# One decoder-layer step: all weight splits on VectorE and ScalarE, sample states loaded on ScalarE's queue, 32x32 products of two block pairs in turn

## The chip, the core and the metric

The kernel runs on one core of a Trainium2 chip. The metric is device time in microseconds (us) of one execution. The core has a matrix engine (TensorE, PE in the profile; its weight loads are PEld), three engines for elementwise work (VectorE or DVE, ScalarE or ACT, GpSimd or POOL) and a queue engine (SyncE, SP). SP and ACT both issue the DMAs of this kernel, each on a hardware queue of its own (q1 and q10 in the profile). Each engine works through its own instructions in order.

## The reference, cut to what matters

One layer of a decoder for a prompt of 256 tokens and 8 sample tokens, which share all weights. So every large product has 264 columns.

```python
h = rmsnorm(x, norm_mix); proj = h @ w_in
pool_out, pool_new = pool_mixer(proj[pool part], ...)          # windows 2/4/8/16
q, k, v = short_conv(proj[qkv part]); o, ssm_new = gated_delta_chunked(q, k, v, g, beta, ssm)
merged = gate_pool * (pool_out @ w_pool_up) + gate_gdn * (gdn_out @ w_gdn_up)
x = x + merged @ w_o
gu = rmsnorm(x, norm_ffn) @ w_gate_up
x = x + (silu(gu[..., :D_FF]) * gu[..., D_FF:]) @ w_down
x = x + (p_l @ w_ple) * sigmoid(x @ w_ple_gate)
# per chunk of gated_delta_chunked: solve (I + strictly lower A) X = rhs, then update the state S
# per sample: S = exp(g) S + k (beta (v - (exp(g) S)^T k))^T ; o = S^T q   (16 heads of 128x128, 8 samples)
```

All data are float32, and all weights (some 300 MB) are read once from HBM.

## The kernel before, in words

**Large products.** Activations lie channel by token. A float32 product is made of three fast ones: each operand is cut into a rounded part and a rest (`wh` and `wl` for a weight block, `hh` and `hl` and so on for activations), and `gemm` (L469) issues `wh*xh`, `wh*xl`, `wl*xh`, each a 128x128 weight tile against 264 columns, into one PSUM bank of tag `acc`. Such a product is called an acc matmul below.

**Weight stream.** `wload` (L429) issues a 512 KB DMA on SP into one of three `wr` buffers. `wsplit` (L441) makes `wh` as a copy on ACT (L355) and `wl` as a subtraction (L339), four buffers of each. `wblock` (L456) keeps up to three split blocks (`LA`) ahead of the matmuls, two more loaded (`LD`). A block feeds 24 acc matmuls. The subtraction of `wl` goes to DVE, except where the test `spare` of `wsplit` sends it to POOL: when the planner's clock of POOL is more than 1.0 us behind that of DVE and DVE's is more than 1.5 us ahead of PE's. Two blocks at the head of the program (in `input_norm`, L631) name POOL outright.

**Order of work.** The order on each engine is written out by the program itself. A planner (`Model`, L34) keeps a clock for each engine from a cost table. Small pieces of work are Python generators; `tick` (after 6 or so acc matmuls) lets the next piece emit its instructions when the planner says that its inputs are there (`at`), unless `behind` finds DVE or ACT more than `room` (3.0 us) ahead of PE. What is emitted is pinned in that order (`pin`). So a planner's estimate that is too early makes the in-order engine wait on the chip, and every later instruction with it.

**Small pieces that the change touches.** `gdn_b` (L1019) inverts the 128x128 triangular blocks of a head group from 32x32 blocks: `px` takes for each of 8 blocks a and for the two block pairs e = 0 and 2 a product of 32x32 blocks (L1060 to L1063), and `py` the same with two products for e = 0 and one for e = 2 (L1069 to L1075). Both write one PSUM bank. Each of these matmuls is float32 and stands as two instructions in the profile. There are four head groups.

`gdn_sample` (L1177) updates the 8 samples' states. A tile `S` holds one head of all samples (128 x 8 x 128, 512 KB) in four buffers. `load` (L1212) issues its DMA on SP; `kqmm` (L1256) waits in the planner for the state and emits 8 small matmuls (16 instructions, `kqp`, L1266); then `pd` products and DVE updates in place (`S`, L345); `swap` (L1217) stores the new state on SP, waits in the planner for the store's landing and calls `load` for the same head of the next group into the same buffer. 16 loads, 16 stores. The pooling mixer (`sw`, `dd`, `db` tiles on DVE) and the products with `w_pool_up` run at the same time.

Of the kernel before, what the change touches and what calls it, by code (L numbers as in the profile page):

```python
# [8 lines left out]
F32 = mybir.dt.float32  # L9
# [21 lines left out]
GH = 4  # L31


class Model:  # L34
# [4 lines left out]
    def __init__(self, nc):  # L39
        self.nc, self.seen, self.bb = nc, 0, None  # L40
        self.T = {e: 0.0 for e in ("PE", "DVE", "Activation", "Pool", "SP")}
        self.ring = 0.0
# [84 lines left out]
    def run(self, floor=0.0):  # L127
# [5 lines left out]
        for k in range(self.seen, len(lst)):  # L133
            i = lst[k]
            eng = str(i.engine).split(".")[-1]
            if eng not in self.T or type(i).__name__.startswith("Bass"):
                continue
            ins = [b for b in map(self.box, i.ins) if b]
            out = [b for b in map(self.box, i.outs) if b]
            at = max([self.T[eng], floor] + [self.ready(b) for b in ins])  # L140
            if type(i).__name__ == "InstDMACopy":
                self.T[eng] = at + 0.06
                n = max(self.free(b) * (b[2] - b[1]) for b in ins + out) * 4
# [10 lines left out]
            held, more = self.cost(i, ins, out)  # L154
            self.T[eng] = at + held
            end = at + held + more
# [7 lines left out]
class Step:  # L164
# [55 lines left out]
    @property  # L220
    def now(self):
        return self.model.T["PE"]

# [214 lines left out]
        self.note(self.splits[-3] if len(self.splits) > 2 else 0.0)  # L438
        self.raws.append((raw, nk, n))

    def wsplit(self, eng=None):  # L441
        self.note()
        raw, nk, n = self.raws.pop(0)
        hi, lo = (self.wp.tile([P, 1024], F32R, tag=t, name=self.nm(t))[:, :nk * n].rearrange("p (k c) -> p k c", c=n)
                  for t in ("wh", "wl"))
        self.nsp += 1
        self.copy(hi, raw)
        T = self.model.T
        spare = T["Pool"] + 1.0 < T["DVE"] and T["DVE"] - T["PE"] > 1.5
        self.sub(lo, raw, hi.bitcast(F32), self.nc.gpsimd if spare else eng)  # L450
        self.npool = getattr(self, "npool", 0) + spare
        self.pre.append((hi, lo))
        self.splits.append(self.note(self.now))

# [176 lines left out]
    def input_norm(self, x, xs):  # L631
        nc = self.nc
        ssq = self.cp.tile([P, 3, 4], F32, name="ssq")
        nc.vector.memset(ssq, 0.0)
        self.xt = self.B3("xT")
        sqj = self.e4("sqj")
        self.xd = self.dp.tile([P, KT, NT], F32, tag="xd", name="xd", bufs=1)
        self.hh = self.B3("hh", F32R)
        self.hl = self.B3("hl", F32R)
        self.xn = None  # L640

        def squares(c):
            cs = slice(c * 512, c * 512 + 512)
            xc = (c % 2) * 512
            self.act(sqj[:, :512], x[:, 0, cs], AF.Square, accum_out=ssq[:, 0, c:c + 1])
            for src, acc in ((x[:, 1, cs], ssq[:, 1, c:c + 1]),
                             (xs[c // 2][:, xc:xc + 512], ssq[:NS, 2, c:c + 1])):
                nc.vector.scalar_tensor_tensor(out=sqj[:src.shape[0], 512:1024], in0=src, scalar=1.0, in1=src,
                                               op0=ALU.mult, op1=ALU.mult, accum_out=acc)

        def turn(k):
            t = self.ps("xt")[:, :NT]
            for b in range(2):
                self.tr(t[:, b * P:(b + 1) * P], x[:, b, k * P:(k + 1) * P])
            cc = (k % 8) * P
            self.tr(t[:, TP:NT], xs[k // 8][:, cc:cc + P])
            if k % 4 == 3:
                nc.vector.tensor_copy(self.xt[:, k], t)
            else:
                self.copy(self.xt[:, k], t)  # L660
        self.turn = turn
        for k in range(12):
            if k in (0, 4, 8):
                squares(k // 4)
            if k == 10:
                squares(3)
            if k == 8:
                self.wsplit(nc.gpsimd)
            turn(k)
        r = self.cp.tile([P, 3], F32, name="rin")  # L670
        nc.vector.tensor_reduce(r, ssq, axis=AX.X, op=ALU.add)
        self.ts(r, r, 1.0 / D, EPS, ALU.mult, ALU.add)
        self.powr(r, r, -0.5)
        self.wsplit(nc.gpsimd)
        turn(12)
        p = self.spread_rows(r)
        turn(13)
        self.rx = self.e1("rx")
        self.copy(self.rx, p)
        for k in range(2):  # L680
            self.htile(k)
        self.wsplit()
        for k in range(2, 4):
            self.htile(k)
# [334 lines left out]
    def gdn_b(self, hg, q, k, v):  # L1019
        nc, gw, o = self.nc, self.gw, self.o  # L1020
        h0 = hg * GH
        G8 = 2 * GH
# [20 lines left out]
        for g in range(2):  # L1043
            for hh in range(2):
                for b in range(2):
                    h = 2 * g + hh
# [10 lines left out]

        sl = lambda i, n: slice(i * n, (i + 1) * n)
        px = self.ps("px").rearrange("p (a c) -> p a c", c=64)
        for e in (0, 2):  # L1060
            E, O = sl(e, 32), sl(e + 1, 32)
            for a in range(G8):
                self.mm(px[O, a, 0:32], A[E, a, O], Tm[E, a, E])  # L1063
        yield -1
        for e in (0, 2):
            O = sl(e + 1, 32)
            nc.vector.tensor_copy(X[O, :, 0:32], px[O, :, 0:32])
        yield -1
        py = self.ps("py").rearrange("p (a c) -> p a c", c=64)  # L1069
        for e in (0, 2):  # L1070
            E, O = sl(e, 32), sl(e + 1, 32)
            for a in range(G8):
                self.mm(py[E, a, 0:32], X[O, a, 0:32], Tt[O, a, O])
                if e == 0:
                    self.mm(py[O, a, 0:32], Tt[O, a, O], X[O, a, 0:32])  # L1075
        yield -1
        for e in (0, 2):
            E, O = sl(e, 32), sl(e + 1, 32)
# [4 lines left out]
        lo, hi = slice(0, 64), slice(64, 128)  # L1083
# [93 lines left out]
    def gdn_sample(self, pool):  # L1177
        nc, o = self.nc, self.o
# [31 lines left out]
        S = {}  # L1210

        def load(hg, h):  # L1212
            S[hg, h] = pool.tile([P, NS, HD], F32, tag="S", name=self.nm("S"), bufs=4)
            self.dma(S[hg, h], self.i["state_ssm"][0, :, hg * GH + h].rearrange("b d e -> d b e"))
        order = list(range(GH - 1, -1, -1))

        def swap(hg, h):  # L1217
            yield self.at(S[hg, h])
            self.dma(o["ssm_s"][0, :, hg * GH + h].rearrange("b d e -> d b e"), S.pop((hg, h)))
            if hg < 3:  # L1220
                yield "stored"
                load(hg + 1, h)
        for h in order:
            load(0, h)
# [31 lines left out]
        def kqmm(hg, h):  # L1256
            while (hg, h) not in S:
                yield -1
            yield self.at(S[hg, h])
            if h == order[0]:  # L1260
                self.kept.clear()
                kqp[0] = self.ps("kqp", True)
            for sl in (2 * h + 1, 2 * h):
                wd = 32 if sl == 7 else 16
                for j in range(4):
                    nc.tensor.matmul(kqp[0][32 * j:32 * j + wd, :P], kq[:, j, 16 * sl:16 * sl + wd],  # L1266
                                     S[hg, h][:, 4 * (sl % 2) + j, :], start=(sl == 7), stop=(sl == 0),
                                     tile_position=(0, 32 * j))
        for h in order:
            yield -1  # L1270
            yield from kqmm(0, h)
        yield -1
        for hg in range(4):
# [38 lines left out]
            for h in order:  # L1312
                for c in range(2):
                    pd = self.ps("pd").rearrange("p (b e) -> p b e", b=4)
                    self.mm(pd, ks[:, hg], rm[:, 4 * c:4 * c + 4, :])
                    if h:
                        mask(h - 1, c)
                    yield -1
                    for b in range(4):
                        bb = 4 * c + b  # L1320
                        n = hg * n32 + h * NS + bb
                        self.stt(S[hg, h][:, bb, :], S[hg, h][:, bb, :], egb[:, n:n + 1], pd[:, b, :])
                    yield 1.2
                self.lane(swap(hg, h))
                if hg < 3 and h < 2:
                    yield from kqmm(hg + 1, h + 2)
            if hg < 3:
                yield -1
                yield from kqmm(hg + 1, 1)
                yield -1  # L1330
                yield from kqmm(hg + 1, 0)
                yield -1
# [451 lines left out]
```

## Time and profile before

| | us |
|---|---|
| median of 3 runs (1927.98 to 1929.02) | 1928.94 |
| profiled execution, whole | 1929.83 |
| its span, first to last instruction | 1928.1 |
| PE busy | 1881.3 |
| DVE busy | 1128.0 |
| ACT busy | 880.9 |
| POOL busy | 521.2 |

The profiled execution is 1.7 us longer than its span and 0.9 us longer than the median of the runs. From about 830 us on (products with `w_gdn_up`, `w_o`, the feed-forward part) PE is busy with hardly a gap up to about 1830 us; the mixer, the gated delta rule and the sample states lie before that. PE's busy time counts overlapping matmuls, so a busy share of 100% says that no gap was seen, not that the array is at its peak.

### The profile page before, as it was taken

The numbers are of one execution on the slowest core, as the hardware profiler recorded it, in microseconds if no ns is written. First come the engines' busy times: TensorE is split into PE (matmuls) and PEld (weight loads), VectorE is DVE, ScalarE is ACT, GpSimd is POOL, SyncE is SP. The second block draws the span as 40 slices with busy tenths as digits, with TensorE's granted clock in tenths as the row PEclk, the third lists the DMA queues.
The fourth block names the chain that finished last, engine by engine and source line by source line (L and its number), as shares of the span: only waits on it lengthen the run. The fifth ranks groups of instructions, "written<-read, shape, count | busy, mean of one in ns | idle before, by whom it ended". The sixth has DMA issues, their size and how long they took to land.

```text
span 1928.1 us, 38025 instructions
## 1 busy us (share of the span) xinstructions
PE 1881.3 (98%) x15700; PEld 1853.6 (96%) x15700; DVE 1128.0 (59%) x1594; ACT 880.9 (46%) x1484; POOL 521.2 (27%) x560
## 2 busy tenths in 40 slices
PE   8999999999999799999999999999999999999997
PEld 6899999999999799999999999999999999999997
DVE  6756466546546866566665555544555545557554
ACT  4565657455544243344444444333444333444444
POOL 3347353622514443322232111100111001122211
PEclk9999999989999899999999999999999999999998
DMA  6556564645656778755655656555555655556553
GB/s 176 153 174 191 135 177 123 189 114 162 183 155 170 222 237 240 219 171 185 220 179 172 193 187 195 185 177 175 176 186 183 191 183 177 175 177 188 161 177 120
DMA packets 368817, 344.92 MB, mean 179 GB/s; under 512 B 26387, under 2 KB 363100, under 8 KB 368628
## 3 DMA queue, kind: packets, MB, share of 16 engines
q1 hardware_dynamic: 355011, 338.82, 58.1%
q10 hardware_dynamic: 13632, 3.67, 0.9%
q8 instruction: 123, 2.02, 0.4%
q14 instruction: 51, 0.41, 0.1%
HBM read 327.28 MB, written 16.03 MB: 178 GB/s over the span
## 4 chain that ended last, share of the span: by engine, by line
PE 85%; DVE 6%; DMA 4%; ACT 2%; issue 2%; POOL 1%; SPq 0%; ACTq 0%; POOLq 0%; DVEq 0%
PE acc L368 79%; DVE wl L339 1%; ACT wh L355 1%; DMA out_dram<-S 1%; DVE sw L336 1%; DMA S<-in_state_ssm_dram 1%; POOL wl L339 1%; DMA wr<-in_w_in_dram 1%; DVE k L345 1%; PE pp L368 0%; PE py L368 0%; PE kv L372 0%; PE px L368 0%; DVE S L345 0%; PE pS L368 0%
## 5 line engine op out<-in xcount | busy, mean ns | idle before, releaser
L339 DVE TENSOR_TENSOR wl<-wr,wh 128x1024 fp32r<-128x1024 f32 (+1 forms) x490 | 620.5, 1279 | 529.8 <-ACT wh L355 528.1
L355 ACT ACTIVATE wh<-wr 128x1024 fp32r<-128x1024 f32 x594 | 611.1, 1049 | 444.2 <-PE acc L368 161.4
L368 PE MATMUL acc<-hh,wh 128*128 128x264 f32 x1664 | 488.3, 293 | 3.7 <-DVE q L345 1.9
L368 PE MATMUL acc<-hl,wh 128*128 128x264 f32 x1664 | 478.2, 287 | 1.2 <-DVE hl L339 1.0
L368 PE MATMUL acc<-hh,wl 128*128 128x264 f32 x1664 | 477.0, 287 | 2.3 <-DVE wl L339 1.5
L339 POOL TENSOR_TENSOR wl<-wr,wh 128x1024 fp32r<-128x1024 f32 x104 | 256.6, 2470 | 705.8 <-ACT wh L355 425.0
L368 PE MATMUL acc<-xnh,wh 128*128 128x264 f32 x1408 | 399.9, 284 | 0.0
L368 PE MATMUL acc<-xnh,wl 128*128 128x264 f32 x1408 | 399.2, 283 | 0.0
L368 PE MATMUL acc<-xnl,wh 128*128 128x264 f32 x1408 | 399.1, 283 | 0.0
L368 PEld LDWEIGHTS acc<-hh,wh 128*128 128x128 f32 x1664 | 318.5, 191 | 8.0 <-issue 2.4
L368 PEld LDWEIGHTS acc<-hl,wh 128*128 128x128 f32 x1664 | 318.8, 192 | 3.7 <-DVE hl L339 2.4
L368 PEld LDWEIGHTS acc<-hh,wl 128*128 128x128 f32 x1664 | 317.7, 191 | 2.7 <-DVE wl L339 1.7
L368 PEld LDWEIGHTS acc<-xnl,wh 128*128 128x128 f32 x1408 | 265.1, 188 | 0.0
L368 PEld LDWEIGHTS acc<-xnh,wh 128*128 128x128 f32 x1408 | 264.8, 188 | 0.1
L368 PEld LDWEIGHTS acc<-xnh,wl 128*128 128x128 f32 x1408 | 264.4, 188 | 0.0
L368 PE MATMUL acc<-hidh,wh 128*128 128x264 f32 x704 | 199.9, 284 | 0.0
L368 PE MATMUL acc<-hidl,wh 128*128 128x264 f32 x704 | 199.6, 283 | 0.0
L368 PE MATMUL acc<-hidh,wl 128*128 128x264 f32 x704 | 199.5, 283 | 0.0
L368 PEld LDWEIGHTS acc<-hidl,wh 128*128 128x128 f32 x704 | 132.5, 188 | 0.0
L368 PEld LDWEIGHTS acc<-hidh,wh 128*128 128x128 f32 x704 | 132.4, 188 | 0.0
L368 PEld LDWEIGHTS acc<-hidh,wl 128*128 128x128 f32 x704 | 132.2, 188 | 0.0
L342 POOL TENSOR_TENSOR gs<-gs,rb 128x264 f32<-128x264 f32 x44 | 33.3, 757 | 365.8 <-ACT gs L352 365.8
(366 smaller groups left out, 2733.8 us busy)
## 6 DMA issues: line engine op xcount, KB each, us to landing
wr<-in_w_in_dram SPq DMA_DIRECT2D x208, 512.0 KB
wr<-in_w_gate_up_dram SPq DMA_DIRECT2D x176, 512.0 KB
wr<-in_w_down_dram SPq DMA_DIRECT2D x88, 512.0 KB
wr<-in_w_gdn_up_dram SPq DMA_DIRECT2D x32, 512.0 KB
wr<-in_w_o_dram SPq DMA_DIRECT2D x32, 512.0 KB
wr<-in_w_ple_gate_dram SPq DMA_DIRECT2D x32, 512.0 KB
S<-in_state_ssm_dram SPq DMA_DIRECT2D x16, 512.0 KB
out_dram<-S SPq DMA_DIRECT2D x16, 512.0 KB
```

What stands on the lines that cost most here:

```text
L336: (eng or self.nc.vector).tensor_tensor(out=out, in0=a, in1=b, op=ALU.add)
L339: (eng or self.nc.vector).tensor_tensor(out=out, in0=a, in1=b, op=ALU.subtract)
L342: (eng or self.nc.vector).tensor_tensor(out=out, in0=a, in1=b, op=ALU.mult)
L345: self.nc.vector.scalar_tensor_tensor(out=out, in0=a, scalar=s, in1=b, op0=op0, op1=op1)
L355: self.nc.scalar.activation(out, a, AF.Copy)
L368: self.nc.tensor.matmul(out, lhsT, rhs, start=start, stop=stop)
```

## The change

Four edits. (1) `wsplit` loses its argument and its test: every `wl` is made on DVE, also the two at the head. (2) `load` of a sample state issues on ACT's queue (`fast`) in place of SP's (`dma`). (3) `kqmm` waits in the planner until 1.0 us after the planner's landing of the state. (4) In `px` and `py` the loops over a and e change places, so that the products of the two block pairs are issued in turn.

```diff
-    def wsplit(self, eng=None):
+    def wsplit(self):
...
         self.copy(hi, raw)
-        T = self.model.T
-        spare = T["Pool"] + 1.0 < T["DVE"] and T["DVE"] - T["PE"] > 1.5
-        self.sub(lo, raw, hi.bitcast(F32), self.nc.gpsimd if spare else eng)
-        self.npool = getattr(self, "npool", 0) + spare
+        self.sub(lo, raw, hi.bitcast(F32))
...
-                self.wsplit(nc.gpsimd)
+                self.wsplit()
...
-        self.wsplit(nc.gpsimd)
+        self.wsplit()
...
-        for e in (0, 2):
-            E, O = sl(e, 32), sl(e + 1, 32)
-            for a in range(G8):
+        for a in range(G8):
+            for e in (0, 2):
+                E, O = sl(e, 32), sl(e + 1, 32)
                 self.mm(px[O, a, 0:32], A[E, a, O], Tm[E, a, E])
...
-        for e in (0, 2):
-            E, O = sl(e, 32), sl(e + 1, 32)
-            for a in range(G8):
+        for a in range(G8):
+            for e in (0, 2):
+                E, O = sl(e, 32), sl(e + 1, 32)
                 self.mm(py[E, a, 0:32], X[O, a, 0:32], Tt[O, a, O])
                 if e == 0:
                     self.mm(py[O, a, 0:32], Tt[O, a, O], X[O, a, 0:32])
...
-            self.dma(S[hg, h], self.i["state_ssm"][0, :, hg * GH + h].rearrange("b d e -> d b e"))
+            self.fast(S[hg, h], self.i["state_ssm"][0, :, hg * GH + h].rearrange("b d e -> d b e"))
...
-            yield self.at(S[hg, h])
+            yield (self.at(S[hg, h])[0] + 1.0,)
```

## Rows read from the trace of the kernel before

**Rows 1.** The page: its head and busy time by engine.
```profile
span 1928.1 us, 38025 instructions
PE 1881.3 (98%) x15700; PEld 1853.6 (96%) x15700; DVE 1128.0 (59%) x1594; ACT 880.9 (46%) x1484; POOL 521.2 (27%) x560
```

**Rows 2.** Windows: length, busy us of PE, PEld, DVE, ACT, POOL, granted clock, DMA share, GB/s.
```profile
1200.00:1300.00 100.00, 100.00 (x828) 100.00 (x827) 50.92 (x53) 37.25 (x38) 4.92 (x2) 1.00 0.61 189
...
30.00:100.00 70.00, 65.46 (x510) 62.41 (x510) 57.00 (x107) 39.81 (x71) 24.77 (x11) 0.95 0.56 153
...
400.00:500.00 100.00, 100.00 (x838) 98.83 (x837) 56.74 (x103) 55.00 (x136) 34.89 (x49) 0.94 0.50 144
...
612.00:670.00 58.00, 46.19 (x367) 43.75 (x366) 52.45 (x87) 18.75 (x32) 32.98 (x21) 0.93 0.64 180
...
690.00:760.00 70.00, 66.91 (x606) 63.61 (x606) 44.42 (x94) 22.69 (x26) 27.38 (x19) 1.00 0.90 270
```

**Rows 3.** Waits of PE, whole span: us in total, times, longest us.
```profile
PE kqp L1266 <- DMA S<-in_state_ssm_dram: 11.1, 7, 3.4
...
PE px L368 <- DVE gone L1054: 3.1, 2, 1.9
PE rb L368 <- POOL rin L381: 2.9, 1, 2.9
...
PE pd L368 <- DVE S L345: 2.3, 2, 1.2
...
PE acc L368 <- DVE q L345: 1.9, 1, 1.9
...
PE acc L368 <- POOL wl L339: 1.7, 2, 0.9
PE acc L368 <- DVE wl L339: 1.5, 1, 1.5
PE gc L368 <- DVE dg L345: 1.4, 1, 1.4
```

**Rows 4.** Groups by line: the weight splits on DVE and on POOL.
```profile
L339 DVE TENSOR_TENSOR wl<-wr,wh 128x1024 fp32r<-128x1024 f32 (+1 forms) x490 | 620.5, 1279 | 529.8 <-ACT wh L355 528.1 <-PE ot L372 1.2
...
L339 POOL TENSOR_TENSOR wl<-wr,wh 128x1024 fp32r<-128x1024 f32 x104 | 256.6, 2470 | 705.8 <-ACT wh L355 425.0 <-PE acc L368 270.4 <-DVE k L336 10.3
```

**Rows 5.** Timeline of POOL, 646 to 656 us.
```profile
646.15 10.01 POOL L339 TENSOR_TENSOR wl<-wr,wh 128x1024 fp32r<-128x1024 f32 x4 [3.02 <-ACT wh L355]
```

**Rows 6.** Timeline of DVE: one kind of addition beside those splits and after.
```profile
648.88 7.56 DVE L336 TENSOR_TENSOR sw<-sw 128x269 f32<-128x269 f32 x3
...
657.86 1.37 DVE L336 TENSOR_TENSOR sw<-sw 128x269 f32<-128x269 f32 x3
```

**Rows 7.** Waits of PE, 600 to 690 us.
```profile
PE kqp L1266 <- DMA S<-in_state_ssm_dram: 8.0, 3, 3.4
```

**Rows 8.** Timeline of SP: issues of the sample states.
```profile
578.99 5.01 SPq L361 DMA_DIRECT2D S<-in_state_ssm_dram  x4
...
651.55 0.50 SPq L361 DMA_DIRECT2D S<-in_state_ssm_dram  x1
```

**Rows 9.** Timeline of PE: the wait for one state.
```profile
657.22 0.63 PE L1266 MATMUL kqp<-S,kq 128*16 128x128 f32 x16 [3.38 <-DMA S<-in_state_ssm_dram]
```

**Rows 10.** Timeline of PE: 32x32 products of the first head group.
```profile
223.28 1.09 PE L368 MATMUL px<-gone,gset 32*32 32x32 f32 x32
...
226.69 0.21 PE L368 MATMUL py<-gset,gone 32*32 32x32 f32 x1
...
227.10 0.21 PE L368 MATMUL py<-gset,gone 32*32 32x32 f32 x2
...
227.22 0.57 PE L368 MATMUL py<-gset,gone 32*32 32x32 f32 x13
```

**Rows 11.** Waits of SP's queue, 560 to 800 us, for landed state stores.
```profile
SPq L361 <- DMA out_dram<-S: 9.4, 6, 2.3
```

**Rows 12.** Timelines of DVE and ACT: last work of the samples, first of the next stage.
```profile
792.12 0.29 DVE L342 TENSOR_TENSOR go<-go,ob 128x128 f32<-128x128 f32 x1
...
819.90 2.29 ACT L355 ACTIVATE gh<-go 128x264 fp32r<-128x264 f32 x7
```

## The prediction

> **What bounds the kernel now.** I read the page first: PE is busy 98% of the span [rows 1]. Busy PE does not say how fast it goes, so the windows come next. A stretch without small work, 1200 to 1300 us, holds 828 matmuls in 100 us at full clock, 0.121 us each [rows 2]; that is the pace of an acc matmul, and nothing in the change touches it. The 594 weight blocks [rows 4] of 24 acc matmuls (a few blocks are smaller) are some 14,200, 1720 us at that pace. The rest of the span, about 210 us, is small matmuls, waits and clock, and nearly all of it lies before 830 us. So the change is worth what it takes from PE's own waits there. The table of PE's waits names them: 11.1 us in seven waits of `kqp` for a sample state's DMA, 2.3 us of `pd` for DVE's update of a state, and 1.9, 1.7, 1.5 and 1.4 us for DVE or for a weight split [rows 3]. Beside them the granted clock is below full in three stretches: 0.95 of 30 to 100 us, 0.94 of 400 to 500 and 0.93 of 612 to 670 [rows 2]. It knows two levels, 2.4 and 1.2 GHz, so such a mean is a piece at 1.2 GHz; each piece follows waits of PE (those of `gc` and `q`, of `px`, of `kqp`).
>
> **All splits on DVE.** 104 splits leave POOL at 2.47 us each and come to DVE, where one takes 1.28 us (means of [rows 4]): 133 us more for an engine that is busy 1128 of 1928 us. That alone would be a load. Against it stands what a POOL split does to DVE. From 646.15 us POOL makes four splits in a row, 10.01 us [rows 5]. Beside them three additions on DVE take 7.56 us, and three of the same shape 1.37 us right after [rows 6]: 2.52 against 0.46 us each, so one split beside such an addition costs DVE 2.06 us, more than the 1.28 us of doing the split itself. DVE gains 0.8 us for each split that meets an operation of this kind, and loses 1.28 us for one that meets none. In 612 to 670 us DVE is busy 52.45 of 58 us [rows 2], so there its delays reach PE.
>
> PE's waits that end with DVE or a split are 2.3, 1.9, 1.7, 1.5 and 1.4 us, 8.8 us together [rows 3]. I take two thirds, -6 us; bounds 0 (DVE is no earlier) and -8.8. With DVE earlier the stretch 30 to 100 us keeps part of its clock: 0.05 of 70 us is 3.5 us, I take half, -1.7, bounds 0 and -3.5. At the head PE waits 2.9 us for `rin` on POOL [rows 3], which stands behind a split there. Taken off POOL, 2.47 us go, but the split's 1.28 us come onto DVE in the same chain: -1.2 us, bounds 0 and -2.9. From 830 to 1830 us PE has no such wait to give back, and DVE at 51 of 100 us has room [rows 2]: 0. The removed test also shifts every planner time behind it, so the emission order changes nearly everywhere. The trace can't show that; I bound it by the longest wait that the present order leaves, 3.4 us [rows 3], either way, and take 0.
>
> **Sample states on ACT's queue, with 1.0 us of margin.** Three of the `kqp` waits, 8.0 us of the 11.1, lie in 600 to 690 us [rows 7]. One read closely: the load is issued at 651.55 us [rows 8], and PE resumes at 657.22 after 3.38 us [rows 9], so landing took 5.7 us. SP comes to such a load late, because weight loads and stores stand ahead of it and wait for `wl` buffers and for the `S` updates, which DVE delays as above. On ACT's queue the load passes those. I take these 8.0 us as gone (5.7 us of flight stay, but the issue moves forward by the wait on SP, and the planner's margin adds 1.0 us) and leave the other four waits, 3.1 us: they lie in 690 to 760 us, where the DMA engines are busy 0.90 at 270 GB/s [rows 2] and a second queue finds no free share. Bounds 0 and -11.1. The clock follows: 0.07 of 58 us is 4.1 us in 612 to 670; I take -4, bounds 0 and -4.1.
>
> The DMA page of the Trainium skill (DMA: Bandwidth & Descriptors, section Issuing engines are not separate DMA queues) speaks against this edit: transfers from all issuing engines run on the same 16 DMA engines, and another issuer saves only the short time of issuing. By that rule the 8.0 and 4 us stay and the sum comes out 12 us longer; that case is a rival below, worked out from the rows alone.
>
> What ACT takes on: 16 issues. The first four kept SP 5.01 us [rows 8], the others about 0.5 us each, 11 us of ACT in all, in stretches where it is busy 18.75 of 58 and 22.69 of 70 us [rows 2]. The twelve later loads also wait for the store of the same buffer to land. On SP that was 9.4 us in six waits, the longest 2.3 [rows 11]; on ACT the same wait now holds what is queued behind it: `wh` copies, hence `wl` and PE, the evacuations of gates and mixer, and the copies `kqs` and `vs` inside the samples' own chain. Cover: three blocks split ahead are 72 matmuls, 72 x 0.121 = 8.7 us of PE; the small copies have none. I take +2 us, bounds 0 and +14.4 (5.01 and 9.4). The margin delays the samples' chain by up to 16 x 1.0 us; its last instruction is at 792.12 us and the next stage starts on it at 819.90 [rows 12], 27.5 us later, so it costs nothing. If the chain slipped by more, PE would pay the rest at the drain there.
>
> **32x32 products in turn.** `px` of the first head group is 32 instructions in 1.09 us [rows 10]; less one duration of about 0.2, 0.9 us of starts, 28 ns each. `py` starts with two products in turn: from 226.69 to 227.22 us 35 instructions start, 15 ns each; its last 13, of one kind, need 0.57 less 0.2, about 29 ns each [rows 10]. In turn, `px` would take 32 x 15 ns = 0.48 us, 0.42 less, and `py` 48 at 10 to 15 ns, 0.2 to 0.4 less. Four head groups: -2.5 to -3.3 us, all on PE, which is the bound; I take -2.8, bounds 0 and -3.3.
>
> The Trainium skill (TensorEngine Tiling (Array Packing), Restrictions and Gotchas, Gotcha 1) says that different row tiles cannot use one PSUM bank at the same time, and here the two pairs are different row tiles into one bank. By it this term is 0 and the sum 2.8 us longer. The row at 227.10 us stands against it: two instructions of `py<-gset,gone` in the place of one, as the second pair's products already start among the first pair's [rows 10].
>
> **Sum.** -6 - 1.7 - 1.2 - 8 - 4 + 2 - 2.8 = -21.7 us. From the profiled execution, 1929.83 us (span 1928.1 and 1.7 around it), that is 1908.1; the median of the runs lay 0.9 below that execution, so the forecast is 1907.2 us.
>
> **The rivals.**
> 1. The states land no sooner. The transfer takes its 5.7 us wherever it is issued, and on a shared set of DMA engines it now also competes with weight loads that it used to follow. For: share 0.90 in 690 to 760 us. Against: 0.64 in 612 to 670 us, where 8.0 us of the waits lie [rows 2, 7]. The 8 and 4 us stay: 1919.2 us.
> 2. ACT's queue is held, and it ends slower. Place: ACT in 580 to 760 us. Price: the first four issues, 5.0 us, and twelve loads at the longest wait seen, 2.3 us, 27.6: together 32.6 us of held ACT in place of my +2, with the state waits staying. It decides once more than 11.7 us of those 32.6 reach PE (the gain left without the states is 9.7, and the +2 is in it). If all do: 1907.2 + 12 - 2 + 32.6 = 1949.8; if half do, 1933.5. For: ACT is in order, and the small copies have no cover. Against: two thirds of ACT's time is free there and the blocks ahead cover 8.7 us.
> 3. All of it goes. All state waits (3.1 more), all waits on DVE (2.8 more), the early clock (1.8 more), the 3.1 us of `px` and with it the piece at 1.2 GHz near 400 us, 0.06 of 100, 6 us [rows 2, 3]: 1907.2 - 16.8 = 1890.4 us. Against: the wait of `px` ends with a transposition behind DMAs that the change leaves alone.
> 4. No change: the new order puts as many new waits as it removes, 1929 us.
>
> **How the numbers follow.** Forecast 0.50, its own range 1899 to 1915 us; rival 1 0.18, rival 2 0.12, rival 3 0.12, no change 0.08. A change under 0.2% (3.9 us) can't be told from none. Faster: 0.50 + 0.18 + 0.12 = 0.80; same 0.08; slower 0.12. The range leaves out rival 2 and no change, 0.20, and takes in rivals 1 and 3: 1890 to 1924 us.
>
> **What would show it.** The group of `wl` on POOL gone, and that on DVE at 594 with a mean near 1.23 us; the `sw` additions near 0.46 us throughout; DVE's busy time not above 1128 us by more than 20. No wait of `kqp` above 1.5 us in 600 to 690 us, and the granted clock above 0.97 there. `px` of 32 instructions in some 0.7 us. Wrong, if the state loads stand as ACT's waits of several us with PE waiting for `wh` right after, or if `kqp` waits as long as before.

## The result and the profile after

The changed kernel takes 1902.94 us (median of four runs, 1899.18 to 1903.12) against 1928.97 us for the kernel before (1927.98 to 1929.02): a ratio of 0.9862, 95% interval 0.9845 to 0.9879, some 26 us less. The forecast was 1907.2 us. The execution that left the profile is the lowest of the four, 1899.18 us; the others took 1902.8 to 1903.1 us, so its windows look a little better than the median does: its mean granted clock was 0.997, that of the other three 0.995. Three lines fell out of the code ahead of the state loop, so L1266 of before is L1263 here.

The page's head and busy times, against [rows 1]:

```profile
span 1897.5 us, 37984 instructions
PE 1863.5 (98%) x15700; PEld 1837.8 (97%) x15700; DVE 1079.6 (57%) x1698; ACT 877.7 (46%) x1482; POOL 258.2 (14%) x456
```

VectorE does 104 instructions more and is busy 48 us less. The groups by line say how (busy us, mean ns). First after, against [rows 4]:

```profile
L339 DVE TENSOR_TENSOR wl<-wr,wh 128x1024 fp32r<-128x1024 f32 x594 | 715.9, 1225 | 534.1 <-ACT wh L355 530.1
L339 DVE TENSOR_TENSOR hidl<-gs,hidh 128x264 fp32r<-128x264 f32 x44 | 16.9, 427 | 0.0
L336 DVE TENSOR_TENSOR sw<-sw 128x269 f32<-128x269 f32 (+2 forms) x12 | 8.2, 682 | 0.4
```

and the last two groups before, which no row ahead of the prediction showed:

```profile
L339 DVE TENSOR_TENSOR hidl<-gs,hidh 128x264 fp32r<-128x264 f32 x44 | 65.5, 1526 | 0.0
L336 DVE TENSOR_TENSOR sw<-sw 128x269 f32<-128x269 f32 (+2 forms) x12 | 15.2, 1269 | 0.4
```

The same subtraction `hidl` takes 427 ns in place of 1526. Had VectorE's own work not become shorter, 104 splits at 1.225 us would have raised its 1128.0 us to 1255.4; it shows 1079.6. So 176 us went from VectorE's other instructions, 1.69 us for each split that left POOL, more than the 1.225 us of doing it. I call this the hold-up.

Windows (length, busy us of PE, PEld, DVE, ACT, POOL with counts, granted clock, DMA share, GB/s), against [rows 2]:

```profile
30.00:100.00 70.00, 68.92 (x562) 66.70 (x561) 51.01 (x108) 37.45 (x69) 0.33 (x11) 1.00 0.59 163
400.00:500.00 100.00, 100.00 (x914) 99.20 (x913) 58.27 (x101) 59.91 (x144) 35.24 (x73) 1.00 0.57 161
612.00:670.00 58.00, 55.80 (x479) 53.85 (x478) 46.04 (x93) 25.73 (x39) 7.04 (x8) 1.00 0.81 238
690.00:760.00 70.00, 66.08 (x603) 62.98 (x602) 41.55 (x84) 23.10 (x28) 12.36 (x12) 1.00 0.90 270
1200.00:1300.00 100.00, 100.00 (x828) 100.00 (x828) 48.60 (x52) 37.01 (x37) 1.51 (x2) 1.00 0.58 179
```

The last line has not moved: 828 matmuls in 100 us, as before. Nor has anything behind the samples: the first matmul of the `w_gdn_up` products (`gh`) starts at 813.1 us in place of 842.8, so 29.7 of the 30.6 us between the two profiled spans are won ahead of it. The gain lies in the three stretches whose clock was below full. Busy time times clock, an estimate of the work done in a window, rose by 6.7 us in 30 to 100, by 6 us in 400 to 500 and by 12.8 us in 612 to 670: 25.5 of the 30.6 us; in 690 to 760 it fell by 0.8. (The windows hold different work at their edges; only the size is meant.)

PE's waits in the whole span, against [rows 3] (us, times, longest us):

```profile
PE kqp L1263 <- DMA S<-in_state_ssm_dram: 5.4, 4, 2.4
...
PE rb L368 <- POOL rin L381: 3.5, 1, 3.5
PE acc L368 <- DVE hl L339: 2.9, 3, 1.9
...
PE px L368 <- DVE gone L349: 1.0, 1, 1.0
...
PE acc L368 <- DVE wl L339: 0.8, 1, 0.8
```

and in 600 to 690 us, against [rows 7]:

```profile
PE kqp L1263 <- DMA S<-in_state_ssm_dram: 1.6, 2, 1.2
```

The waits of `pd`, `q`, `gc` and of the splits on POOL are gone from the table; the one of `rb` has grown.

### The profile page after: what moved, and what is told of

Same layout as the page of the kernel before. It is cut to its first block, busy times and chain, and to the rows that moved or that the text cites. A ratio compares the mean times of both kernels' runs of the same rounds, so it can differ in the third digit from the quotient of the medians.

```text
span 1897.5 us, 37984 instructions
## 1 busy us (share of the span) xinstructions
PE 1863.5 (98%) x15700; PEld 1837.8 (97%) x15700; DVE 1079.6 (57%) x1698; ACT 877.7 (46%) x1482; POOL 258.2 (14%) x456
## 4 chain that ended last, share of the span: by engine, by line
PE 88%; DMA 4%; DVE 3%; issue 2%; ACT 2%; POOL 0%; ACTq 0%; SPq 0%; POOLq 0%; DVEq 0%
PE acc L368 82%; DVE wl L339 2%; DMA S<-in_state_ssm_dram 1%; ACT wh L355 1%; DMA out_dram<-S 1%; DMA wr<-in_w_ple_gate_dram 1%; PE pp L368 1%; DVE S L345 1%; PE kv L372 1%; PE kqp L1263 0%; PE po L368 0%; PE pS L368 0%; PE pu L368 0%; PE px L368 0%; PE py L368 0%
## 5 line engine op out<-in xcount | busy, mean ns | idle before, releaser
L339 DVE TENSOR_TENSOR wl<-wr,wh 128x1024 fp32r<-128x1024 f32 x594 | 715.9, 1225 | 534.1 <-ACT wh L355 530.1
L368 PEld LDWEIGHTS acc<-hh,wh 128*128 128x128 f32 x1664 | 314.1, 189 | 5.8 <-issue 2.2
L368 PEld LDWEIGHTS acc<-hl,wh 128*128 128x128 f32 x1664 | 314.3, 189 | 5.1 <-DVE hl L339 4.1
L368 PEld LDWEIGHTS acc<-hh,wl 128*128 128x128 f32 x1664 | 313.3, 188 | 1.0 <-DVE wl L339 1.0
L336 POOL TENSOR_TENSOR ss<-ss,sst 128x264 f32<-128x264 f32 x28 | 21.2, 758 | 395.4 <-ACT sst L352 269.7
```

Source lines behind the costliest of these rows:

```text
L336: (eng or self.nc.vector).tensor_tensor(out=out, in0=a, in1=b, op=ALU.add)
L339: (eng or self.nc.vector).tensor_tensor(out=out, in0=a, in1=b, op=ALU.subtract)
L368: self.nc.tensor.matmul(out, lhsT, rhs, start=start, stop=stop)
```

## Experiments

All times stand beside runs of the kernel before on the same chip (four sets, their medians 1927.0 to 1928.6 us); ratios are to those. The changed kernel stands at 0.9862. In short:

```
run                    what is in it                          us       ratio (95% interval)
split_only             edit 1 (splits)                        1915.12  0.9936 (0.9921 to 0.9950)
act_only               edit 2 (states on ACT's queue)         1935.87  1.0041 (1.0022 to 1.0060)
margin_only            edit 3 (1.0 us of margin)              1926.14  0.9989 (0.9979 to 0.9999)
turn_only              edit 4 (products in turn)              1923.03  0.9972 (0.9959 to 0.9984)
split_turn             edits 1, 4                             1912.01  0.9915 (0.9900 to 0.9930)
no_act                 edits 1, 3, 4                          1902.83  0.9867 (0.9852 to 0.9882)
no_margin              edits 1, 2, 4                          1902.41  0.9870 (0.9854 to 0.9887)
no_split               edits 2, 3, 4                          1925.14  0.9988 (0.9979 to 0.9998)
```

**Each edit alone.** Edit 1, the kernel before with

```
-        spare = T["Pool"] + 1.0 < T["DVE"] and T["DVE"] - T["PE"] > 1.5
-        self.sub(lo, raw, hi.bitcast(F32), self.nc.gpsimd if spare else eng)
+        self.sub(lo, raw, hi.bitcast(F32))
```

> The kernel before with the first edit alone: every wl on VectorE. Theory 1 (a GpSimd split holds up VectorE operations with two SBUF inputs beside it, VectorE is then late, and PE, the state updates and the state stores with it): about 14 us faster, 1915 us; the sw additions near 0.46 us throughout, PE's waits for VectorE or a split in 30 to 100 and 612 to 670 us mostly gone, VectorE busy below 1128 us. Theory 2 (the states' waits come from the order on SP's queue and the splits matter little): at most 6 us faster, and PE still waits about 8 us for kqp in 600 to 690 us.

Measured 1915.12 us. The clock of 30 to 100 us is back, that of 612 to 670 partly (to be held against [rows 2]), and the waits for landed stores on SP [rows 11] grew:

```profile
30.00:100.00 70.00, 69.23 (x564) 67.34 (x563) 51.11 (x108) 37.48 (x69) 0.00 (x0) 1.00 0.58 164
...
612.00:670.00 58.00, 51.97 (x417) 50.59 (x417) 42.04 (x87) 26.11 (x42) 5.84 (x5) 0.97 0.74 219
```

```profile
SPq L361 <- DMA out_dram<-S: 20.4, 6, 4.7
```

VectorE is busy 1077.4 us, as theory 1 has it, and the `sw` additions take 0.56 us in the mean. No wait of `kqp` is left in 600 to 690 us, so theory 2 falls; but the waits for states have moved more than gone (PE's longest wait in 600 to 690 us, then in 690 to 760 us, where they were 3.1 us before):

```profile
PE acc L368 <- DVE pob L345: 4.6, 1, 4.6
```

```profile
PE kqp L1263 <- DMA S<-in_state_ssm_dram: 9.4, 4, 4.0
```

The 400 to 500 us window, 0.94 before, is at full clock here too, and no wait of `px` is left [rows 3].

Edit 2 alone:

```
-            self.dma(S[hg, h], ...)
+            self.fast(S[hg, h], ...)
```

> The kernel before with the second edit alone: sample states loaded on ScalarE's queue, no margin, splits on GpSimd as before. Theory 1: at most 5 us faster, about 1925 us; the kqp waits in 600 to 690 us shrink by less than half, since the stores that the loads wait for are still late. Theory 2: about 12 us faster, 1917 us, kqp waits there under 2 us and the clock at 2.4 GHz. Theory 3 (ScalarE is held by the landing of stores and PE pays): slower than before.

Measured 1935.87 us: slower by 0.4%, as theory 3 has it. The trace has the mechanism of rival 2: ScalarE stands before a weight split until a store has landed, and behind the first of these waits PE waits 3.3 us for that split. The waits for states have left 600 to 690 us here as well (0.6 us there) and come later. (`ptp` is a transposition of the pooling mixer; ACT's waits, then PE's.)

```profile
ACT wh L355 <- DMA out_dram<-S: 12.4, 3, 7.3
```

```profile
PE kqp L1266 <- DMA S<-in_state_ssm_dram: 6.7, 4, 4.5
...
PE ptp L372 <- DVE S L345: 3.5, 1, 3.5
PE acc L368 <- ACT wh L355: 3.3, 1, 3.3
```

```profile
612.00:690.00 78.00, 65.48 (x518) 62.29 (x517) 65.71 (x113) 30.25 (x53) 36.63 (x25) 0.91 0.61 182
690.00:760.00 70.00, 63.83 (x553) 60.88 (x555) 42.35 (x101) 20.34 (x23) 31.58 (x24) 0.96 0.79 242
```

Edit 3 alone:

```
-            yield self.at(S[hg, h])
+            yield (self.at(S[hg, h])[0] + 1.0,)
```

> The kernel before with the third edit alone: the planner waits 1.0 us longer for each state. Theory 1: within 4 us of before, since the longest waits are 3.4 us and the margin moves the matmuls by 1.0. Theory 4 (PE's order alone is too early and the margin is what removes the waits): about 8 us faster, 1921 us, and kqp waits of at most 3 us in the whole span.

Measured 1926.14 us, 0.1% less than before: under what can be told from none. The longest wait of `kqp` is 5.2 us, so theory 4 falls.

Edit 4 alone (`px` and `py` alike):

```
-        for e in (0, 2):
-            for a in range(G8):
+        for a in range(G8):
+            for e in (0, 2):
```

> The kernel before with the fourth edit alone: 32x32 products of the two block pairs in turn. Theory 1 (products of different row tiles start in turn at about 15 ns, also into one PSUM bank): px about 0.4 us and py 0.2 to 0.4 us shorter per head group, 2.5 to 3.3 us together, 1926 us; if the piece at 1.2 GHz near 400 us goes too, 6 us more. Rival (row tiles that share a PSUM bank do not overlap): px still 0.9 us from first to last start, no change in time.

Measured 1923.03 us, 0.28% less. The window 400 to 500 us runs at full clock (0.94 before), 30 to 100 us stays at 0.95. As with edit 1 alone, PE has no wait for `px` left. With edit 2 or edit 3 alone those waits stay (2.8 and 2.6 us) and so do slow pieces, but at another place: 0.95 and 0.93 of 500 to 575 us, where the kernel before had 1.00. So the slow pieces show in the kernels that keep these waits, though not at the same place in each execution.

**Each edit taken back from the changed kernel.** One line, or for the splits the test and the two head splits, as it was before.

> The changed kernel with the sample states loaded on SP's queue again; splits on VectorE, margin and products in turn stay. The second edit alone made the kernel before 7.9 us slower. Theory A (that edit helps once the stores land when the planner says, which the splits on VectorE bring about): slower than the changed kernel by 5 us or more, 1908 us or above, with kqp waits for states above 8 us. Theory B (that edit never helps, and the changed kernel is fast in spite of it): 1903 us or less.

> The changed kernel without the 1.0 us of margin. Theory A (with loads that start on time the flight is a little longer than the planner's, and the margin covers it): 3 to 6 us slower than the changed kernel, about 1907 us, with more than 5.4 us of kqp waits. Theory B (the margin does nothing): 1903 us, with the same waits.

> The changed kernel with the test of before again, so that some hundred splits are on GpSimd; loads on ScalarE, margin and products in turn stay. Theory 1 and A (the splits on VectorE are the main part, and the loads on ScalarE need them): at least 20 us slower than the changed kernel, 1923 to 1930 us, with ScalarE held by landing stores and the clock below full in 612 to 690 us. Theory 2 (the three other edits carry it): about 1910 us.

Without edit 2 the time is 1902.83 us, without edit 3 1902.41: neither is missed. (Without edit 3 `kqp` waits 7.4 us, above 5.4 as theory A has it, but the time is theory B's.) Without edit 1 it is 1925.14: all but 3 us of the gain is gone; the clock of 612 to 690 us is 0.91, ScalarE stands 3.1 us before landed stores and PE 2.5 us for a `wh` behind one of them. In the kernel without edit 2 the states on SP do wait for landed stores, but PE hardly notices (first SP's waits, then PE's in 560 to 830 us):

```profile
SPq L361 <- DMA out_dram<-S: 14.8, 7, 3.1
```

```profile
PE acc L368 <- DVE pob L345: 3.5, 1, 3.5
PE kqp L1263 <- DMA S<-in_state_ssm_dram: 2.0, 4, 0.9
```

Each alone could be left out, then. The next run leaves out both.

> The kernel before with the first and the fourth edit alone: all splits on VectorE, products of the block pairs in turn; sample states loaded on SP's queue and no margin ahead of their products. Theory 1 (the second and the third edit add nothing once the splits have moved): 1901 to 1905. Rival (each of the two is made good by the other, since either alone could be left out of the changed kernel without loss): SP's issues wait for landed stores again, 10 us or more of such waits and more than 6 us of waits of kqp for a state, and the time is 1908 to 1915.

Measured 1912.01 us; the rival holds. The interval, 0.9900 to 0.9930, does not meet that of the changed kernel, 0.9845 to 0.9879: 9 us are lost where either edit alone lost none. SP's and PE's waits of this kernel:

```profile
SPq L361 <- DMA out_dram<-S: 20.3, 6, 4.8
```

```profile
PE kqp L1263 <- DMA S<-in_state_ssm_dram: 8.4, 3, 3.9
...
PE acc L368 <- DVE pob L345: 3.7, 1, 3.7
```

```profile
612.00:670.00 58.00, 52.59 (x421) 50.72 (x419) 40.66 (x83) 24.56 (x39) 4.16 (x4) 0.94 0.71 211
...
690.00:760.00 70.00, 62.24 (x517) 59.11 (x516) 43.02 (x99) 19.70 (x23) 17.93 (x17) 0.93 0.73 217
```

Edits 2 and 3 stand in for each other. The queue issues the loads with no wait on SP; the margin places the products later, and with it alone PE waits 2.0 us for states in place of 8.4, though SP is held for 14.8 us. Of the 8.4 us, 7.8 lie in 690 to 760 us and none in 600 to 690.

**Why splits on POOL cost so much.** Two theories: VectorE's instructions that run beside a POOL split are held up (theory 1), or the low half simply comes later, 2.47 us on POOL. Three kernels add useless work on POOL to the changed kernel behind every sixth split; nothing is left out. The first two differ in that work alone (both in short form):

```
+            nc.gpsimd.tensor_copy(dut, wh[:, 0:1])       # a copy of one column
+            3 x nc.gpsimd.tensor_tensor(dum, ones, ones, subtract)   # 128x300
+        or  7 x nc.gpsimd.memset(dum, 0.0)                           # 128x300
```

> The changed kernel, and behind every sixth weight split a useless piece of work on POOL, three subtractions 128x300 of two operands in SBUF (about 2.1 us by the 2.35 us of a 128x1024 split there, some 98 times, as many as the splits that POOL did before). No result is read and nothing waits for it; the order of the instructions on the other engines stays. Theory 1 (the splits on POOL cost time because VectorE's instructions that run beside them are held up): VectorE's busy time grows from 1080 us by 80 to 160 us, the mean of wl on VectorE from 1.23 us to 1.4 or more, and the time grows by 8 to 25 us, to 1911 to 1928. Rival (the splits on POOL cost time because their own low half came later, 2.35 us in place of 1.23): nothing late is added here, so the time stays within 3 us of 1903.

> As the run with useless subtractions, but the useless work behind every sixth split is seven memsets 128x300 on POOL, which read nothing from SBUF and keep POOL busy for about as long. Theory 1 (VectorE is held up by POOL's reading of two operands in SBUF): the time stays within 3 us of 1903, VectorE's busy time within 20 us of 1080. Rival (any work of POOL holds VectorE up, or POOL itself is late): the time grows as with the subtractions, by 8 us or more.

Measured 1930.59 us (ratio 1.0018, 1.0008 to 1.0028) with subtractions and 1926.14 (0.9995, 0.9984 to 1.0006) with memsets. VectorE's busy time went the way of theory 1, but not by its size (the pages, subtractions first):

```profile
PE 1875.4 (97%) x15700; PEld 1847.8 (96%) x15700; DVE 1124.0 (58%) x1698; ACT 876.8 (45%) x1482; POOL 591.2 (31%) x852
```

```profile
PE 1871.4 (97%) x15700; PEld 1844.8 (96%) x15700; DVE 1079.7 (56%) x1698; ACT 877.4 (46%) x1482; POOL 554.7 (29%) x1248
```

With subtractions it grew by 44 us where 80 to 160 were expected, and the mean of `wl` to 1266 ns where 1400 were; with memsets it stayed. POOL's useless work, 333 us with subtractions, thus held VectorE up far less than its 256.6 us of splits had, 176 us. The times fit theory 1 in neither run, 1930.59 above its range and 1926.14 far from 1903, and the reason is a fault of mine: the small copy reads `wh`, so its buffer stays taken until POOL comes to the copy, and the next split waits. (ACT's waits of the kernel with memsets.)

```profile
ACT wh L355 <- POOL dut L459: 34.3, 3, 13.1
```

That "nothing waits for it" was wrong. What the pair still gives is its difference: 44 us more on VectorE, 4.4 us more time, the held buffer being common to both (33.9 us of this wait with subtractions, 34.3 with memsets). A third kernel lets ScalarE copy the column, and POOL reads that copy:

```
+            nc.scalar.copy(dut[:, j], wh[:, 0:1])
+            nc.gpsimd.tensor_copy(duc, dut[:, j])
+            2 x nc.gpsimd.tensor_tensor(dum, ones, ones, subtract)   # 128x704
```

> The changed kernel with useless subtractions on POOL that hold no buffer of the weights. In the two runs with useless work before, POOL's small copy read wh itself, and ScalarE then waited for that copy before it could write the next wh (34.3 us, 3 times, in the one with memsets). Here ScalarE copies one column of wh into a tile of its own right behind the split (99 times) and POOL reads that; then POOL does two subtractions 128x704 of two operands in SBUF at each place (about 3.2 us). The order on the other engines stays, apart from those 99 copies. Theory 1 (VectorE's instructions, held up by POOL's reading beside them, have a price of their own: 4.4 us for 44 us more of VectorE's busy time, by the difference of those two runs): VectorE's busy time grows by 50 to 150 us, the time by 5 to 15 us to 1908 to 1918. Rival (all that those runs lost came from the held wh): VectorE's busy time grows as much, and the time stays within 2.5 us of 1903.

Measured 1920.03 us, but spread from 1914.51 to 1928.72; ratio 0.9967, 0.9951 to 0.9983. The profiled execution took 1914.95 us, near the lower end.

```profile
PE 1870.6 (98%) x15700; PEld 1842.2 (96%) x15700; DVE 1165.9 (61%) x1698; ACT 894.9 (47%) x1581; POOL 654.1 (34%) x753
```

```profile
L339 DVE TENSOR_TENSOR wl<-wr,wh 128x1024 fp32r<-128x1024 f32 x594 | 777.0, 1329 | 484.2 <-ACT wh L355 483.1 <-PE yt L372 0.3
```

```profile
PE acc L368 <- DVE wl L339: 4.6, 5, 1.5
```

```profile
30.00:100.00 70.00, 66.59 (x534) 63.96 (x534) 53.84 (x98) 35.97 (x67) 10.89 (x9) 1.00 0.52 149
...
612.00:670.00 58.00, 52.98 (x427) 50.66 (x426) 48.27 (x91) 25.04 (x44) 21.65 (x19) 0.97 0.65 192
...
690.00:760.00 70.00, 65.03 (x550) 62.18 (x550) 47.40 (x102) 21.64 (x28) 32.55 (x26) 0.95 0.78 231
```

No `wh` copy of ScalarE waits for POOL now, no weight data comes late through POOL, and still 17 us are lost. The three windows hold 28, 52 and 53 matmuls fewer than in the changed kernel; the first two are stretches where the change had won. The rival, 2.5 us at most, falls. The 17 us lie above theory 1's 5 to 15, and are not the price of VectorE alone: POOL's own work (`rm`, `gm`) also stands behind the useless work, ScalarE makes 99 copies more (19.0 us), and it stands 8.7 us in two waits before landed stores of states, which the changed kernel does not. How the loss divides among these was not separated. So the three runs show that VectorE is held up by POOL's reading, and that the hold-up costs time; how edit 1's own gain divides between the hold-up, the low halves that came later on POOL and the order of emission, which shifts with the splits, they don't show.

**The head.** The changed kernel with the two splits in the input norm on POOL again; every other instruction stays in its order.

```
-                self.wsplit()
+                self.wsplit(nc.gpsimd)
...
-        self.wsplit()
+        self.wsplit(nc.gpsimd)
         turn(12)
```

> The changed kernel with the first two weight splits, those inside the input norm, on POOL again as before; every other instruction stays in its order on its engine. Theory 1 (in the changed kernel the power on POOL for rin, 1.76 us beside a split on VectorE against 0.85 us before, delays the whole kernel): rb starts at 18.25 us again in place of 19.54, and the time falls by 1.0 to 1.5 us to about 1901.6. Rival (the head is made up later, the weights' arrival sets it): rb at 18.25, but the time stays within 0.5 us of 1902.9.

`rb` started at 18.39 us, 1.15 earlier than in the changed kernel; the time was 1900.43 us (1898.16 to 1904.44), ratio 0.9861, 0.9844 to 0.9877. The head is as theory 1 has it, but whether the 1.15 us arrive at the end can't be told at this spread. It is no better than the changed kernel by any margin that these runs show.

## Why the prediction was right, and which terms were not

The total was right (26.0 us less against 21.7 forecast), and so was the place: PE's waits and clock between 30 and 830 us, nothing after. The terms can be laid beside a chain of runs, splits first, then the products, then the two state edits (medians of three sets of runs, from 1928.59; before differs by up to 1.6 us between sets, so no step is known to better than 2 or 3 us):

```
                              forecast                      measured
splits (-6 -1.7 -1.2)         -8.9                          -13.5   to 1915.12
products in turn              -2.8                           -3.1   to 1912.01
states (-8 -4 +2)            -10.0                           -9.1   to 1902.94
```

**Splits: undersized, by some 4.6 us** (by the ratio, 9.6 to 15.2 us went where I had 8.9). I priced a split on POOL by the one pair of rows that I had [rows 5, 6], 2.06 us of hold-up against 1.28 of work, and then counted only those waits of PE that name DVE or a split. The hold-up was general (1.69 us per split, `hidl` 1526 to 427 ns). The clock of 30 to 100 us came back whole, where I took half. The piece at 1.2 GHz near 400 us, 6 us by my own figures, stands at nothing in my sum: I left it to rival 3, because the wait of `px` ahead of it ends with a transposition that I took to be untouched. With edit 1 alone that wait is gone and 400 to 500 us are at full clock. The rows of a single trace did not show that this wait hung on the splits. The rule of the Trainium skill (SBUF — State Buffer, section Who interferes with whom) is that VectorE and GpSimd share one pair of ports and that the pair is an exclusive lock: VectorE's instructions with two inputs in SBUF meet POOL's reads, not an instruction of POOL that only writes. The two runs with useless work agree: 1124.0 us of VectorE beside subtractions, 1079.7 beside memsets, 1079.6 with neither.

**Head: wrong sign.** I took -1.2 us for `rin` freed of the split ahead of it on POOL. But [rows 3] name POOL's power as what ends the wait, and POOL had stood idle for 1.98 us ahead of it, waiting for VectorE: the split did not delay it. In the changed kernel it runs beside a split on VectorE: 1.76 us, and 0.85 us with that split on POOL (timelines of POOL, kernel before, changed kernel and the one with the head's splits on POOL):

```profile
17.34 0.85 POOL L381 TENSOR_TENSOR rin<-rin,mhalf 128x3 f32<-128x3 f32 x1 [1.98 <-DVE rin L349]
```

```profile
17.72 1.76 POOL L381 TENSOR_TENSOR rin<-rin,mhalf 128x3 f32<-128x3 f32 x1 [16.34 <-DVE rin L349]
```

```profile
17.49 0.85 POOL L381 TENSOR_TENSOR rin<-rin,mhalf 128x3 f32<-128x3 f32 x1 [1.25 <-DVE rin L349]
```

The hold-up that I had charged to VectorE goes both ways. `rb` came at 19.54 us in place of 18.25.

**States: right in size, wrong in place and reason.** The 6.4 us of `kqp` waits that went in 600 to 690 us (8.0 to 1.6) look like my term, and I gave them to ACT's queue. But edit 1 alone leaves none of them there, so they are no worth of the state edits. What these edits take away, once the splits have moved, lies in 690 to 760 us, where I had left the waits standing for want of a free share of the DMA engines: 7.8 us with edits 1 and 4, and in the changed kernel:

```profile
PE kqp L1263 <- DMA S<-in_state_ssm_dram: 3.8, 2, 2.4
```

Beside it go a wait for `pob` (3.7 us to 0.4) and the lower clock (0.94 of 612 to 670 us and 0.93 of 690 to 760, both 1.00 in the changed kernel). That -9.1 us comes so near to -10 is therefore in part luck. The 1.00 in 612 to 670 us belongs to the fastest execution: the kernels without edit 2 and without edit 3, profiled at 1903 us, show 0.94 there. I also gave nothing to the margin, and either edit does it alone once the splits have moved. With the splits still on POOL the two together did nearly nothing: 1923.03 with the products alone, 1925.14 with the products and both state edits. So this term hangs on the first one.

By the Trainium skill (DMA: Bandwidth & Descriptors, section Issuing engines are not separate DMA queues) another issuing engine saves only the short time of issuing. Beside the margin that agrees: 1902.83 us without edit 2, 1902.94 with it. Without the margin it does not: 1912.01 us without edit 2, 1902.41 with it. What the queue changes is in which engine's order the load waits for the store, and that showed: 20.3 us of it on SP with edits 1 and 4, 12.4 us on ScalarE with edit 2 alone, no such row on either in the changed kernel.

**ACT's load: the mechanism of rival 2 is real, but not here.** Alone the edit is slower. In the changed kernel no wait of ScalarE for a landed store of a state is left; with its head's splits on POOL there is one of 4.5 us, so it is near. With the hundred splits back on POOL the row returns (3.1 us in two waits); without the margin it stays absent. So, in one execution of each, the moved splits take these waits away and the margin is not needed for it.

**Products in turn: right.** `px` of the first head group, against [rows 10]:

```profile
228.08 0.69 PE L368 MATMUL px<-gone,gset 32*32 32x32 f32 x32
```

and the first and the last of `py`:

```profile
231.80 0.21 PE L368 MATMUL py<-gset,gone 32*32 32x32 f32 x1
...
232.31 0.19 PE L368 MATMUL py<-gset,gone 32*32 32x32 f32 x1
```

`px` takes 0.69 us in place of 1.09, as forecast; `py`, from 231.80 to 232.50, 0.70 in place of 1.10 (226.69 to 227.79 before). Six of the eight such groups, two in each head group, give 0.38 to 0.41 us each. The two of the third head group ran in the piece at 1.2 GHz before, in 1.49 and 1.73 us, and take 0.69 and 0.70 now; at 0.40 for each of the eight it would be 3.2 us. By the page on TensorEngine Tiling (Array Packing) of the Trainium skill, Gotcha 1 of Restrictions and Gotchas, different row tiles could not work into one PSUM bank at once and nothing would have been gained; the measurement differs from it, and decides. Alone the edit gave more, 0.28%, and the clock near 400 us came back with it; behind edit 1 that was already won.

**Signs that I had named.** `wl` at 594 and 1.225 us: right. VectorE not above 1148 us: far below. No `kqp` wait above 1.5 us in 600 to 690 us, clock above 0.97: right in the profiled execution. The `sw` additions at 0.46 us throughout: wrong, mean 0.68, since POOL keeps other work that reads two operands: two additions that start at 607.97 us take 2.35 us beside two `rm` products on POOL (607.55 to 610.03 us). The margin hidden by the slack ahead of the next stage: no run shows a cost of it. The piece at 1.2 GHz near 400 us, which I left to rival 3: gone, with edit 1 alone and with edit 4 alone too.

## What to carry to other kernels

Before moving work to an idle POOL, compare the mean of VectorE's instructions beside it and away from it: here each split moved there saved VectorE 1.2 us and cost it 1.7. Where edits meet in one chain, neither "alone" nor "taken back" gives an edit's worth: one that is slower alone (+0.4%) and not missed when taken back was still one of two that between them hold 9 us. And a load that has to wait for a store belongs on a queue where little that matters stands behind it, or its use far enough behind it (12.4 us of such waits on ScalarE cost time here, 14.8 us on SP with the margin hardly any). When a wait has gone from one window, look for it in the next before counting it as won.

## What the runs showed that I had not expected

- A tiny POOL instruction, 128x3, was held up as well: 1.76 us beside a 1.23 us split on VectorE, 0.85 us where VectorE did nothing beside it.
- One small read on a late engine holds a buffer for all: a copy of one column on POOL kept ScalarE waiting for 34.3 us in three places.
- The spread of a kernel's runs went with the clock: of the run with useless work that holds no buffer, the execution of 1914.51 us had a mean granted clock of 0.995 and the one of 1928.72 us 0.989, with the same instructions in the same order.
